# Norms of q and k taken in two steps and spread over reordered projection groups, in a transformer block on one core

## The chip, the core and the metric

The kernel runs on one core of one Trainium2 chip. The core has a matrix engine (TensorE, PE in the profile; its weight loads are PEld), a vector engine (VectorE, DVE), a scalar engine for activation functions (ScalarE, ACT), a general engine (GpSimd, POOL) and a queue that issues transfers (SyncE, SP). Each engine works through its own list of instructions in order and waits on semaphores. The metric is the device time of one execution in microseconds, the median of several runs.

## What is computed

One block with 256 tokens of width 2048, a context of 256 tokens, everything in float32:

```python
h  = modulate(rms_norm(x, norm1_w), sh1, sc1)          # hc the same from ctx
q, k, v, ft, pool, sv, sb, sc = split(h @ w_in)        # 5632 columns: 3 x 1024, then 5 x 512
kc, vc = split(hc @ w_in[:, 1024:3072])
q, k, kc = (rms_norm(per head of 128, weight) for each)
branches = (neighbourhood_attention(q, k, v, kc, vc, rpb), fourier_mix(ft),
            pool_mix(pool), short_conv_mix(sv, sb, sc))
x = x + g1 * (sum_i sigmoid(h @ w_gate[i]) * (branches[i] @ w_branch[i])) @ w_o
x = x + g2 * swiglu(modulate(rms_norm(x, norm2_w), sh2, sc2))
```

There are eight attention heads of width 128. The six modulation vectors come from `silu(c) @ w_mod + b_mod`.

## The kernel before

Every large product is made of three matmuls: weights and activations are split into a high and a low half (`split`), the high half cast by ScalarE (L90), the low half subtracted by VectorE (L91), and `mm3` adds high x high, high x low and low x high (L95 to L97). A weight tile of 128 x 1024 float32 (512 KB) holds two rows of 128 weights for 512 columns, or other shapes of this size. There are five buffers for raw weights and three each for the high and the low halves.

The input projection `h @ w_in` runs over the 16 blocks of 128 input rows in chunks of 1, 1, 2, 4, 4 and 4. In each chunk `in_groups` goes over the columns and adds its part into the tiles `xin[0..10]` (512 columns each: 0 and 1 are q, 2 and 3 are k, 4 and 5 are v, 6 Fourier, 7 pooling, 8 to 10 convolution) and, for columns 2 to 5 alone, into `cin[2..5]` for the context. In the last chunk `last(g)` finishes one group of 512 columns: two weight tiles (in the profile in_0 and in_2, their halves in_0h, in_0l, in_2h, in_2l), 24 matmuls for x (in_psx) and, for groups 2 to 5, 24 more for the context (in_psc). A finished product is added into its tile by VectorE (L301). `last` also calls `pump` twice, which issues one job of the queue `jobs` for every second call: a load of a modulation weight tile and, three jobs later, its sum on VectorE (`mod_sum`, L386).

`qk_norm` normalizes one tile of 4 heads: a square on ScalarE (L447), a sum per head on VectorE (L450), a small scale and offset on VectorE and the power -1/2 on GpSimd (`rstd_of`, L243 and L244), and the scaling of the whole tile on VectorE (L452). It is called for q0, k0 and ck0 (heads 0 to 3) after the groups 0, 2 and 4, and for q1, k1 and ck1 (heads 4 to 7) after group 10.

`bias_pair` fills the position bias of two heads by eight small transfers that GpSimd issues, and adds a mask on GpSimd (L470). `head(h, bias)` is one attention head: transposes of q, k and ck, scores, softmax, transposes of the weights, and the product with v. Heads 0 to 3 are called among the groups, heads 4 to 7 among the gates that follow. `fourier` (L537 to L545) comes after the groups, then `gate(0, 1, ...)`, whose weights are the tiles gt.

All tiles of 128 x 1024 that live longer (inputs, scratch for squares, the heads' tiles, biases) share 34 buffers, `U`. The order of each engine's list isn't the order of the program: a planner goes through the program with its own costs of each instruction, prefers what stands earlier in the program among the instructions that it takes to be ready, and hands out buffers as they come free. `tc.issue_after(ins)` adds an order without a wait: what is issued in the block comes behind `ins` on its engine. `state["low"]` is the last subtraction of `split` (L91) that the program has written so far.

Of the kernel before, what the change touches and what calls it, by code (L numbers as in the profile page):

```python
# [8 lines left out]
F32 = mybir.dt.float32  # L9
F32R = mybir.dt.float32r  # L10
AF = mybir.ActivationFunctionType
ALU = mybir.AluOpType
# [3 lines left out]
P = 128  # L16
# [26 lines left out]
def block_kernel(ctx: ExitStack, tc: tile.TileContext, t_in, out):  # L43
    nc = tc.nc
# [6 lines left out]
    sm = ctx.enter_context(tc.tile_pool(name="sm", bufs=1))  # L51
# [3 lines left out]
    def U(name, dtype=F32):  # L55
        return up.tile([P, 1024], dtype, tag="u", name=name, bufs=NU)
# [7 lines left out]
    def tr_ps(name):  # L64
        return pst.tile([P, 512], F32, tag="tr", name=name)
# [61 lines left out]
    def tsplit(hi, lo, src):  # L127
        nc.scalar.copy(hi, src)
        nc.vector.tensor_tensor(lo, src, hi.bitcast(F32), ALU.subtract)
# [3 lines left out]
    state = {"tick": 0, "every": 2, "hold": False, "low": None}  # L133

    def pump():
        state["tick"] += 1
        if state["tick"] % state["every"] == 0 and jobs and not state["hold"]:
            jobs.pop(0)()
# [102 lines left out]
    def rstd_of(ss, out_, n, scale):  # L241

        nc.vector.tensor_scalar(ss, ss, scale, EPS, ALU.mult, ALU.add)  # L243
        nc.gpsimd.tensor_tensor(out_, ss, mhalf.to_broadcast([P, n]), ALU.pow)  # L244
# [46 lines left out]
    xin = [None] * 11  # L291
    cin = [None] * 6
# [10 lines left out]
    def in_groups(kt0, nk, c0, cw):  # L303

        first = kt0 == 0

        kn, cn = min(nk, 2), 1024 // min(nk, 2)
        done = {}
        for c in range(c0, c0 + cw, cn):
            pw = min(cn, c0 + cw - c)  # L310
            for ka in range(0, nk, kn):
                raw = raw_tile(f"in_w{kt0}_{c}_{ka}")
                rv = raw[:, :kn * pw].rearrange("p (k f) -> p k f", k=kn)
                r = (kt0 + ka) * P
                nc.sync.dma_start(
                    rv, w_in[r:r + kn * P, c:c + pw].rearrange("(k p) f -> p k f", p=P))
                wh, wl = split(rv, f"in{kt0}_{c}_{ka}", (kn, pw))
                for gc in range(0, pw, 512):
                    done.setdefault(c + gc, []).append(
                        (ka, ka + kn, wh[:, :, gc:gc + 512], wl[:, :, gc:gc + 512]))  # L320
        for gc, parts in done.items():
            g = gc // 512
            for which in ("x", "c") if 2 <= g < 6 else ("x",):
                store = xin if which == "x" else cin
                if first:
                    store[g] = U(f"in_{which}{g}").rearrange("p (t f) -> p t f", t=NT)
                for t in range(NT):
                    ps = acc_ps(f"in_ps{which}{kt0}_{g}_{t}")
                    sl = slice(t * P, (t + 1) * P)
                    for ka, kb, wh, wl in parts:  # L330
                        for kk in range(ka, kb):
                            hi, lo = hx(kt0 + kk) if which == "x" else hc[kt0 + kk]
                            mm3(ps, hi[:, sl], lo[:, sl], wh[:, kk - ka, :], wl[:, kk - ka, :],
                                kk == 0, kk == nk - 1)
                    evict(ps, store[g][:, t, :], first, (g + t) % 2)
# [105 lines left out]

    def qk_norm(buf, name):
        v3 = buf.rearrange("p t (h d) -> p (t h) d", d=P)
        scr = U(f"sq_{name}")
        nc.scalar.activation(scr, buf.rearrange("p t f -> p (t f)"), AF.Square)  # L447
        ss = sm.tile([P, 8], F32, tag="ssh", name=f"ssh_{name}", bufs=2)
        rs = sm.tile([P, 8], F32, tag="rsh", name=f"rsh_{name}", bufs=2)
        nc.vector.tensor_reduce(ss, scr.rearrange("p (h d) -> p h d", d=P), AX.X, ALU.add)  # L450
        rstd_of(ss, rs, 8, 1.0 / P)
        nc.vector.tensor_tensor(v3, v3, rs.unsqueeze(2).to_broadcast([P, 8, P]), ALU.mult)  # L452

    rpb = t_in["rpb"]
    wmask = const.tile([P, GRID_W], F32, name="wmask")
# [2 lines left out]
    def bias_pair(h0):  # L458


        b = U(f"bias{h0}").rearrange("p (h t f) -> p h t f", h=2, t=NT)
        for i in range(2):
            for r in range(ROWS):
                src = bass.AP(rpb.tensor, rpb.offset + (h0 + i) * 15 * 31 + (7 - r) * 31 - 48,
                              [[1, GRID_W], [31, ROWS], [1, GRID_W]])
                p0 = (r % 2) * GRID_W
                nc.gpsimd.dma_start(
                    b[p0:p0 + GRID_W, i, r // 2, :].rearrange("p (a c) -> p a c", a=ROWS), src)
        bv = b.rearrange("p h t (a c) -> p (h t a) c", a=ROWS)
        nc.gpsimd.tensor_tensor(  # L470
            bv, bv, wmask.unsqueeze(1).to_broadcast([P, 2 * NT * ROWS, GRID_W]), ALU.add)
        return b

    def reverse(v):

        return v.rearrange("p (r c) -> p r c", c=GRID_W)[:, :, ::-1]

    def head(h, bias):
        g, o_ = h // 4, (h % 4) * P

        qf = U(f"qf{h}")
        pa, pb = tr_ps(f"qk_ps{h}"), tr_ps(f"ck_ps{h}")
        for t in range(NT):
            nc.tensor.transpose(pa[:, t * P:(t + 1) * P], xin[g][:, t, o_:o_ + P], ident)
            nc.tensor.transpose(pa[:, S + t * P:S + (t + 1) * P], xin[2 + g][:, t, o_:o_ + P], ident)
            nc.tensor.transpose(pb[:, t * P:(t + 1) * P], cin[2 + g][:, t, o_:o_ + P], ident)

        nc.scalar.mul(qf[:, 0:S].rearrange("p (r c) -> p r c", c=GRID_W), reverse(pa[:, 0:S]), qks[:, 0:1])
        nc.vector.tensor_scalar(qf[:, S:2 * S], pa[:, S:2 * S], qks[:, 1:2], None, ALU.mult)
        nc.scalar.mul(qf[:, 2 * S:3 * S], pb[:, :S], qks[:, 1:2])  # L490
        p_ = U(f"p{h}").rearrange("p (t f) -> p t f", t=NT)
        pT = U(f"pT{h}").rearrange("p (j q) -> p j q", j=4)
        for t in range(NT):
            sl = slice(t * P, (t + 1) * P)
            s_ps = tr_ps(f"s_ps{h}{t}")
            nc.tensor.matmul(s_ps, lhsT=qf[:, sl], rhs=qf[:, S:3 * S], start=True, stop=True)
            nc.vector.tensor_tensor(s_ps[:, :S], s_ps[:, :S], bias[:, t, :], ALU.add)
            nmx = sm.tile([P, 1], F32, tag="nmx", name=f"nmx{h}{t}", bufs=2)
            nc.vector.tensor_reduce(nmx, s_ps, AX.X, ALU.max, negate=True)
            sm_ = sm.tile([P, 1], F32, tag="sum", name=f"sum{h}{t}", bufs=2)  # L500
            nc.scalar.activation(p_[:, t, :], s_ps, AF.Exp, bias=nmx, scale=1.0, accum_out=sm_)
            rc = sm.tile([P, 1], F32, tag="rc", name=f"rc{h}{t}", bufs=2)
            nc.vector.reciprocal(rc, sm_)
            nc.vector.tensor_scalar(p_[:, t, :], p_[:, t, :], rc, None, ALU.mult)
            p_ps = tr_ps(f"p_ps{h}{t}")
            for j in range(4):
                nc.tensor.transpose(p_ps[:, j * P:(j + 1) * P], p_[:, t, j * P:(j + 1) * P], ident)
            nc.scalar.copy(pT[:, :, sl], p_ps.rearrange("p (j q) -> p j q", j=4))
        o_ps = tr_ps(f"o_ps{h}")
        for j in range(4):  # L510
            v_ = xin[4 + g] if j < 2 else cin[4 + g]
            nc.tensor.matmul(o_ps[:, :S], lhsT=v_[:, j % 2, o_:o_ + P], rhs=pT[:, j, :],
                             start=j == 0, stop=j == 3)
        hi, lo = bT[0][h // 4]
        tsplit(hi[:, h % 4, :].rearrange("p (r c) -> p r c", c=GRID_W),
               lo[:, h % 4, :].rearrange("p (r c) -> p r c", c=GRID_W), reverse(o_ps[:, :S]))
# [146 lines left out]
    def last(g):  # L663
        in_groups(starts[-1], CHUNKS[-1], g * 512, 512)
        for _ in range(2):
            pump()

    bt_tiles(0, 2)
    for g in (0, 2, 4):
        last(g)  # L670
    qk_norm(xin[0], "q0")
    qk_norm(xin[2], "k0")
    qk_norm(cin[2], "ck0")
    bias = bias_pair(0)
    head(0, bias[:, 0])
    last(1)
    head(1, bias[:, 1])
    last(3)
    bias = bias_pair(2)
    head(2, bias[:, 0])  # L680
    last(5)
    head(3, bias[:, 1])
    for g in (6, 7, 8, 9, 10):
        last(g)
        if g == LOAD_AT:
            load_tables()
    qk_norm(xin[1], "q1")
    qk_norm(xin[3], "k1")
    qk_norm(cin[3], "ck1")
    bias = bias_pair(4)  # L690
    fourier()
    load_pool()
# [192 lines left out]
```

## Time and profile before

| | us |
|---|---|
| median of 3 runs (lowest, highest) | 1789.87 (1789.64, 1791.45) |
| the profiled execution | 1791.95 |
| its span, from the first instruction to the last | 1790.2 |
| TensorE busy in the span | 1746.6 (98%) |
| VectorE busy | 1139.6 (64%) |
| ScalarE busy | 741.5 (41%) |
| GpSimd busy | 63.5 (4%) |

The mean clock that was granted to TensorE is 0.996 of full speed. In the rows of a timeline the first number is the start, the second the duration, both in us; then engine, line, operation, the tile written and the tiles read, and in brackets how long the engine had been idle before and what ended that. Durations of neighbouring instructions overlap by about 0.1 us on VectorE and by more on TensorE, where matmuls are pipelined: there the distance of the starts (0.23 us for a matmul of 512 columns) is what one costs. The last chunk's groups lie between 325.9 and 435.2 us.

### The profile page before, as it was taken

How to read it: one execution, taken by the hardware profiler on the slowest of the kernel's cores; microseconds unless marked ns; L12 is line 12 of the kernel's file. 1: busy time of each engine (PE TensorE's matmuls, PEld its weight loads, DVE VectorE, ACT ScalarE, POOL GpSimd, SP SyncE). 2: the span in 40 equal slices, each digit the busy share in tenths (PEclk: the TensorE clock that was granted, in tenths of full speed). 3: DMA queues.
4: the chain of work that ended last, by engine and by line, in shares of the span. 5: the costliest groups of instructions: out<-in, count | busy, mean ns of one | idle time of the engine just before them, and what ended most of it. 6: DMA issues, size and time to landing. Idle time of an engine off the chain costs nothing.

```text
span 1790.2 us, 20871 instructions
## 1 busy us (share of the span) xinstructions
PE 1746.6 (98%) x7874; PEld 1397.0 (78%) x7874; DVE 1139.6 (64%) x1310; ACT 741.5 (41%) x870; POOL 63.5 (4%) x78
## 2 busy tenths in 40 slices
PE   5999999998999999999999999999999999999998
PEld 3676877776777888888888778888888888888887
DVE  5875656677778677777777567776544444454544
ACT  5322322334455444444444454444444444433342
POOL 0000000223010000000000000000000000000000
PEclk9999999999999999999999999999999999999999
DMA  9786675667776788888998548887556666565663
GB/s 315 251 283 224 194 252 178 138 131 185 235 188 226 259 275 290 286 288 262 308 319 286 185 153 281 283 283 227 182 188 188 189 190 189 190 201 197 208 203 116
DMA packets 212872, 404.06 MB, mean 226 GB/s; under 512 B 14178, under 2 KB 53012, under 8 KB 212772
## 3 DMA queue, kind: packets, MB, share of 16 engines
q1 hardware_dynamic: 209732, 396.37, 68.1%
q0 software_dynamic: 1888, 4.26, 2.4%
q10 hardware_dynamic: 1152, 2.10, 0.3%
q8 instruction: 62, 1.02, 0.2%
q14 instruction: 38, 0.31, 0.0%
HBM read 400.58 MB, written 2.10 MB: 225 GB/s over the span
## 4 chain that ended last, share of the span: by engine, by line
PE 72%; issue 2%; DVE 1%; DMA 0%; ACT 0%; POOL 0%; POOLq 0%; DVEq 0%; ACTq 0%
PE gt_ps L96 6%; PE gt_ps L97 6%; PE gt_ps L95 6%; PE fu_ps L97 4%; PE fu_ps L95 4%; PE fu_ps L96 4%; PE dn_ps L97 4%; PE dn_ps L95 4%; PE dn_ps L96 4%; PE fg_ps L95 4%; PE fg_ps L97 4%; PE fg_ps L96 4%; PE br_ps L95 2%; PE br_ps L96 2%; PE br_ps L97 2%
## 5 line engine op out<-in xcount | busy, mean ns | idle before, releaser
L386 DVE SCALAR_TENSOR_TENSOR macc<-mod,cs,macc 128x1024 f32<-128x1024 f32 x128 | 163.8, 1280 | 0.0
L301 DVE TENSOR_TENSOR in_x<-in_x,in_psx 128x512 f32<-128x512 f32 x110 | 74.2, 684 | 40.3 <-PE in_psx L97 39.9
L90 ACT CAST in_2h<-in_w 128x1024 fp32r<-128x1024 f32 x33 | 34.7, 1052 | 148.5 <-PE in_psc L97 94.6
L95 PE MATMUL in_psx<-in_0h,hxh 128*128 128x512 f32 x220 | 89.1, 412 | 1.3 <-ACT hxh L281 1.0
L90 ACT CAST in_0h<-in_w 128x1024 fp32r<-128x1024 f32 (+1 forms) x56 | 57.8, 1035 | 77.3 <-PE in_psc L97 36.9
L96 PE MATMUL in_psx<-in_0l,hxh 128*128 128x512 f32 x220 | 87.1, 399 | 0.0
L97 PE MATMUL in_psx<-in_0h,hxl 128*128 128x512 f32 x220 | 86.6, 396 | 0.0
L91 DVE TENSOR_TENSOR in_0l<-in_w,in_0h 128x1024 fp32r<-128x1024 f32 (+1 forms) x56 | 69.5, 1241 | 3.4 <-ACT in_0h L90 3.3
L91 DVE TENSOR_TENSOR in_2l<-in_w,in_2h 128x1024 fp32r<-128x1024 f32 x33 | 40.4, 1224 | 34.3 <-ACT in_2h L90 32.5
L95 PEld LDWEIGHTS in_psx<-in_0h,hxh 128*128 128x128 f32 x220 | 41.5, 191 | 24.9 <-issue 6.7
L96 PE MATMUL in_psx<-in_2l,hxh 128*128 128x512 f32 x132 | 53.4, 405 | 3.7 <-DVE in_2l L91 3.7
L95 PE MATMUL in_psx<-in_2h,hxh 128*128 128x512 f32 x132 | 53.4, 404 | 0.0
L97 PE MATMUL in_psx<-in_2h,hxl 128*128 128x512 f32 x132 | 51.9, 393 | 0.0
L96 PEld LDWEIGHTS in_psx<-in_0l,hxh 128*128 128x128 f32 x220 | 42.1, 191 | 10.7 <-issue 1.7
L97 PEld LDWEIGHTS in_psx<-in_0h,hxl 128*128 128x128 f32 x220 | 42.2, 192 | 9.1
L209 PE MATMUL mod_ps<-mod_w,cst 128*32 128x512 f32 (+1 forms) x288 | 40.9, 580 | 4.6 <-DMA mod_w<-in_w_mod 4.6
L301 DVE TENSOR_TENSOR in_c<-in_c,in_psc 128x512 f32<-128x512 f32 x40 | 27.2, 686 | 22.7 <-PE in_psc L97 22.6
L91 DVE TENSOR_TENSOR gt_0l<-gt_w,gt_0h 128x1024 fp32r<-128x1024 f32 x16 | 19.6, 1224 | 25.9 <-ACT gt_0h L90 25.9
L96 PEld LDWEIGHTS in_psx<-in_2l,hxh 128*128 128x128 f32 x132 | 24.9, 189 | 11.7 <-DVE in_2l L91 4.5
L91 DVE TENSOR_TENSOR br_0l<-br_w,br_0h 128x1024 fp32r<-128x1024 f32 x16 | 19.6, 1225 | 22.3 <-ACT br_0h L90 22.3
L91 DVE TENSOR_TENSOR gt_12l<-gt_w,gt_12h 128x1024 fp32r<-128x1024 f32 x16 | 19.6, 1225 | 20.3 <-ACT gt_12h L90 20.3
L96 PE MATMUL in_psc<-in_0l,hch 128*128 128x512 f32 x80 | 31.2, 390 | 0.0
(657 smaller groups left out, 5171.4 us busy)
## 6 DMA issues: line engine op xcount, KB each, us to landing
mod<-in_w_mod SPq DMA_DIRECT2D x128, 512.0 KB, 5.5
gt_w<-in_w_gate SPq DMA_DIRECT2D x128, 512.0 KB, 5.5
fg_w<-in_w_ffn_gate SPq DMA_DIRECT2D x88, 512.0 KB, 4.2
fu_w<-in_w_ffn_up SPq DMA_DIRECT2D x88, 512.0 KB, 3.5
dn_w<-in_w_ffn_down SPq DMA_DIRECT2D x88, 512.0 KB, 4.7
in_w<-in_w_in SPq DMA_DIRECT2D x87, 512.0 KB, 5.1
mod_w<-in_w_mod SPq DMA_DIRECT2D x128, 256.0 KB, 5.2
wo_w<-in_w_o SPq DMA_DIRECT2D x32, 512.0 KB, 5.3
```

The costliest lines, as they stand in the source:

```text
L90: nc.scalar.copy(hv, src)
L91: state["low"] = nc.vector.tensor_tensor(lv, src, hv.bitcast(F32), ALU.subtract)
L95: nc.tensor.matmul(ps, lhsT=xh, rhs=wh, start=first, stop=False)
L96: nc.tensor.matmul(ps, lhsT=xh, rhs=wl, start=False, stop=False)
L97: nc.tensor.matmul(ps, lhsT=xl, rhs=wh, start=False, stop=last)
L209: nc.tensor.matmul(ps[32 * j:32 * j + 32, :2 * nf], lhsT=cst[:, kk, :], rhs=rvs[j // kn][:, j % kn, :, :].rearrange("p s f -> p (s f)"), s ...
L301: nc.vector.tensor_tensor(dst, dst, ps, ALU.add)
L386: nc.vector.scalar_tensor_tensor(macc[m][h_], mod_raw.pop((m, kk, h_)), cs[:, 0, kk:kk + 1], macc[m][h_], ALU.mult, ALU.add)
```

## The change

`qk_norm` becomes two functions. `qk_rstd` does the square, the sums and the power; `qk_scale` scales the tile, ordered behind the last low-half subtraction written so far. The small tiles get three buffers in place of two. The groups come in the order 2, 0, 4, 3, 1, 5, 6 to 10 in place of 0, 2, 4, 1, 3, 5, 6 to 10. The norms of both sets are spread over the groups, the first bias pair is asked for earlier, and the heads 0 to 3 come one group later in the program.

```diff
-    def qk_norm(buf, name):
-        v3 = buf.rearrange("p t (h d) -> p (t h) d", d=P)
+    def qk_rstd(buf, name):
         scr = U(f"sq_{name}")
         nc.scalar.activation(scr, buf.rearrange("p t f -> p (t f)"), AF.Square)
-        ss = sm.tile([P, 8], F32, tag="ssh", name=f"ssh_{name}", bufs=2)
-        rs = sm.tile([P, 8], F32, tag="rsh", name=f"rsh_{name}", bufs=2)
+        ss = sm.tile([P, 8], F32, tag="ssh", name=f"ssh_{name}", bufs=3)
+        rs = sm.tile([P, 8], F32, tag="rsh", name=f"rsh_{name}", bufs=3)
         nc.vector.tensor_reduce(ss, scr.rearrange("p (h d) -> p h d", d=P), AX.X, ALU.add)
         rstd_of(ss, rs, 8, 1.0 / P)
-        nc.vector.tensor_tensor(v3, v3, rs.unsqueeze(2).to_broadcast([P, 8, P]), ALU.mult)
+        return buf, rs
+
+    def qk_scale(buf, rs):
+        v3 = buf.rearrange("p t (h d) -> p (t h) d", d=P)
+        with tc.issue_after(state["low"].ins):
+            nc.vector.tensor_tensor(v3, v3, rs.unsqueeze(2).to_broadcast([P, 8, P]), ALU.mult)
...
     bt_tiles(0, 2)
-    for g in (0, 2, 4):
-        last(g)
-    qk_norm(xin[0], "q0")
-    qk_norm(xin[2], "k0")
-    qk_norm(cin[2], "ck0")
+    last(2)
+    k0, ck0 = qk_rstd(xin[2], "k0"), qk_rstd(cin[2], "ck0")
     bias = bias_pair(0)
+    last(0)
+    qk_scale(*k0)
+    q0 = qk_rstd(xin[0], "q0")
+    qk_scale(*ck0)
+    last(4)
+    qk_scale(*q0)
+    last(3)
     head(0, bias[:, 0])
+    k1, ck1 = qk_rstd(xin[3], "k1"), qk_rstd(cin[3], "ck1")
     last(1)
+    qk_scale(*k1)
     head(1, bias[:, 1])
-    last(3)
+    q1 = qk_rstd(xin[1], "q1")
     bias = bias_pair(2)
+    last(5)
+    qk_scale(*ck1)
     head(2, bias[:, 0])
-    last(5)
+    last(6)
+    qk_scale(*q1)
     head(3, bias[:, 1])
-    for g in (6, 7, 8, 9, 10):
+    for g in (7, 8, 9, 10):
         last(g)
         if g == LOAD_AT:
             load_tables()
-    qk_norm(xin[1], "q1")
-    qk_norm(xin[3], "k1")
-    qk_norm(cin[3], "ck1")
     bias = bias_pair(4)
     fourier()
```

## The prediction

> **What bounds the kernel now.** I read the page first (engines' shares), then who waited for whom on TensorE (PE) around the norms, then the clock by stretches, then the timelines of VectorE (DVE), GpSimd (POOL) and ScalarE (ACT) in the two places that stood out.
>
> ```profile
> span 1790.2 us, 20871 instructions
> ...
> PE 1746.6 (98%) x7874; PEld 1397.0 (78%) x7874; DVE 1139.6 (64%) x1310; ACT 741.5 (41%) x870; POOL 63.5 (4%) x78
> ```
>
> PE is busy for 98% of the span, so a change that removes no matmul can only win time in which PE stands idle or runs at a lower clock. Between 325 and 460 us, where both sets of norms lie, PE waited so:
>
> ```profile
> PE in_psx L96 <- DVE in_2l L91: 3.7, 2, 3.1
> PE ft_o L543 <- ACT ft_a L540: 2.7, 1, 2.7
> PE gt_ps L96 <- DVE gt_0l L91: 2.6, 1, 2.6
> ```
>
> Columns: total us, number of waits, longest. So there are four waits: 3.1 us (3.11 in the timeline), 0.56, 2.73 and 2.60. The clock behind them, by stretches (length, busy us of PE, PEld, DVE, ACT, POOL, granted clock, DMA share, GB/s):
>
> ```profile
> 325.92:331.36 5.44, 5.44 (x26) 4.50 (x25) 3.65 (x5) 2.11 (x2) 0.00 (x0) 1.00 0.65 200
> 348.50:352.00 3.50, 3.50 (x11) 2.67 (x10) 1.93 (x4) 0.00 (x0) 1.42 (x1) 0.51 1.21 37
> 435.20:441.70 6.50, 3.77 (x11) 2.14 (x10) 1.22 (x2) 1.53 (x2) 2.90 (x2) 0.92 0.59 211
> 441.70:452.20 10.50, 7.90 (x16) 4.35 (x15) 7.88 (x7) 1.33 (x3) 5.84 (x3) 0.72 0.16 53
> 1041.30:1043.00 1.70, 1.70 (x8) 1.52 (x9) 0.51 (x2) 0.76 (x2) 0.00 (x0) 0.54 0.73 242
> 1043.00:1046.00 3.00, 3.00 (x16) 2.82 (x15) 2.23 (x7) 2.12 (x6) 0.00 (x0) 0.69 0.30 114
> ```
>
> The first row is one projection group on x (5.44 us); a group on x and context takes two such passes. The second row lies just behind the 3.11 us wait: clock 0.51 for 3.50 us, which loses 3.50 x 0.49 = 1.7 us more. The third and fourth lose 6.50 x 0.08 + 10.50 x 0.28 = 3.5 us. The last two are far away, behind this wait:
>
> ```profile
> 1041.29 1.02 PE L766 MATMUL h_tp<-ident,xn 128*128 128x128 f32 x4 [2.08 <-ACT xn L759]
> ```
>
> They lose 1.70 x 0.46 + 3.00 x 0.31 = 1.7 us. So a single wait of 2.08 us already brings the slow clock, and a wait costs its length and about 1.7 us.
>
> **First place.** DVE's timeline, from the scaling of q on:
>
> ```profile
> 337.92 1.23 DVE L452 TENSOR_TENSOR in_x<-in_x,rsh_q 128x1024 f32<-128x1024 f32 x1 [1.79 <-POOL rsh_q L244]
> 339.06 0.68 DVE L301 TENSOR_TENSOR in_x<-in_x,in_psx 128x512 f32<-128x512 f32 x1
> 340.88 1.22 DVE L450 TENSOR_REDUCE ssh_k<-sq_k 128x8 f32<-128x1024 f32 x1 [1.13 <-ACT sq_k L447]
> 342.01 0.68 DVE L301 TENSOR_TENSOR in_c<-in_c,in_psc 128x512 f32<-128x512 f32 x1
> 342.61 0.17 DVE L243 TENSOR_SCALAR ssh_k<-ssh_k 128x8 f32<-128x8 f32 x1
> 344.53 1.22 DVE L452 TENSOR_TENSOR in_x<-in_x,rsh_k 128x1024 f32<-128x1024 f32 x1 [1.76 <-POOL rsh_k L244]
> 345.67 0.68 DVE L301 TENSOR_TENSOR in_c<-in_c,in_psc 128x512 f32<-128x512 f32 x1
> 346.27 1.22 DVE L91 TENSOR_TENSOR in_2l<-in_w,in_2h 128x1024 fp32r<-128x1024 f32 x1
> ```
>
> DVE works in order. The scaling (L452) stands idle 1.76 us for POOL's power, and behind it stands in_2l, the low half of the second weight pair of the group that PE is in. An undisturbed in_2l has this margin (DVE's row, then PE's use of it):
>
> ```profile
> 331.28 1.23 DVE L91 TENSOR_TENSOR in_2l<-in_w,in_2h 128x1024 fp32r<-128x1024 f32 x1 [1.76 <-ACT in_2h L90]
> ```
> ```profile
> 332.94 0.39 PE L96 MATMUL in_psx<-in_2l,hxh 128*128 128x512 f32 x1
> ```
>
> It ends at 331.28 + 1.23 = 332.51, PE wants it at 332.94: 0.43 us to spare. Anything longer ahead of it is an idle PE.
>
> **Second place.** POOL, DVE and ACT at the end of the projections:
>
> ```profile
> 438.80 2.34 POOL L470 TENSOR_TENSOR bias<-bias,wmask 128x1024 f32<-128x1024 f32 x1 [5.41 <-issue]
> 441.10 1.66 POOL L244 TENSOR_TENSOR rsh_k<-ssh_k,mhalf 128x8 f32<-128x8 f32 x1
> 442.74 2.33 POOL L575 TENSOR_TENSOR in_x<-in_x,in_x 128x1024 f32<-128x1024 f32 x1
> ```
> ```profile
> 442.79 3.36 DVE L452 TENSOR_TENSOR in_x<-in_x,rsh_k 128x1024 f32<-128x1024 f32 x1 [6.37 <-POOL rsh_k L244]
> 446.08 0.16 DVE L243 TENSOR_SCALAR ssh_ck<-ssh_ck 128x8 f32<-128x8 f32 x1
> 446.15 1.21 DVE L91 TENSOR_TENSOR gt_0l<-gt_w,gt_0h 128x1024 fp32r<-128x1024 f32 x1
> ```
> ```profile
> 438.69 1.04 ACT L90 CAST gt_4h<-gt_w 128x1024 fp32r<-128x1024 f32 x1 [3.59 <-DMA gt_w<-in_w_gate]
> 439.64 0.58 ACT L540 COPY ft_a<-ft_ps 128x512 f32<-128x512 f32 x1
> ```
>
> k1's power stands in POOL's queue behind the masking of a bias pair, which started only after 5.41 us of idling ("issue": no releaser is seen; I read it as the pair's transfers); DVE's scaling waits 6.37 us for it, and gt_0l, which PE needs, stands behind the scaling. That is PE's 2.60. The 2.73 is another matter: ft_a's copy stands on ACT behind a cast whose weights had not landed.
>
> **The change, part by part.** *Counts.* The six norms keep all their instructions: six squares, reductions (1.22, row of 340.88), small scalings (0.17), powers (1.66, row of 441.10) and scalings (1.23). A square is
>
> ```profile
> L447 ACT ACTIVATE sq_q<-in_x x2: 1053/1058/1063, 333.1 to 423.3; 128x1024 f32<-128x1024 f32 x2
> ```
>
> Nothing is added or removed, so 0 us by count; one more buffer for the two small tiles costs no time, bounded by one power's wait (1.76) either way.
>
> *First set split.* k0 now takes q0's old place in time: its x pass ends first, its power is ready near 337.9 as q0's was. Its scaling must come behind in_2l of group 0, due at about 336.7 (0.08 before group 0 starts at 336.80) and done at 337.9. So DVE finds the power there: no wait. ck0 and q0 follow a group later. I count the first place as removed: -3.11 - 1.7 = -4.81. Bounds: 0 (it returns, first rival) and -4.81.
>
> *Second set moved.* k1, q1 and ck1 are reduced and scaled among groups 1, 5 and 6. Their three powers leave the queue ahead of bias pair 4's masking, and gt_0l no longer stands behind a scaling. Of the second place, 2.73 + 2.60 + 3.5 = 8.8 us in all, I leave the ft_a wait and its slow clock (2.73 + 1.7 = 4.4): the gain is -4.4. Bounds: 0 and -8.8.
>
> By the Trainium skill, "TensorE: Matmul & The Clock Gate", section "What's actually happening", PE falls to half clock after at least one idle window of about 3.4 us. By that rule the 2.73 left alone would bring no slow clock, the gain here would be 8.8 - 2.73 = 6.1 and the time 1.7 us lower. The trace differs, 2.08 us of idling having sufficed at 1041.29, so I stay with 4.4.
>
> *Heads later.* Head 0 starts behind group 3 in place of group 4, so one 10.9 us group later. The four heads are a chain that took from
>
> ```profile
> 358.14 0.27 PE L484 MATMUL qk_ps<-ident,in_x 128*128 128x128 f32 x1
> ```
> ```profile
> 430.47 1.03 PE L512 MATMUL o_ps<-pT,in_c 128*128 128x256 f32 x4
> ```
>
> that is 73.3 us. Starting at 364.0 (325.92 + 7 x 5.44) it ends near 437, while the projections, 4.8 + 0.6 us shorter, would end near 430 where they ended at 435.2 (the start of the third stretch above, with the Fourier step). The 7 us of overhang lie beside the first gate's matmuls, which need no head: 16 weight rows x 2 token halves x 3 = 96, four passes of 24, so 4 x 5.44 = 22 us. I take 0; without that cover it is +7.
>
> *bias_pair(0).* Its eight transfers and the mask are issued five passes (27 us) before head 0 instead of directly before. Before, mask and split met:
>
> ```profile
> 360.48 3.30 POOL L470 TENSOR_TENSOR bias<-bias,wmask 128x1024 f32<-128x1024 f32 x1 [6.39 <-DMA bias<-in_rpb]
> ```
> ```profile
> 361.43 3.43 DVE L91 TENSOR_TENSOR in_0l<-in_w,in_0h 128x1024 fp32r<-128x1024 f32 x1
> ```
>
> A subtraction of 1.22 took 3.43, and the 0.56 us wait came of it. The mask will meet some other DVE instruction, so I take 0, between -0.56 and 2.2 - 0.43 = +1.8 (if it is an in_2l). The Trainium skill, "Advanced Engine Details and Errata", section "Mode Summary", has GpSimd and VectorE blocking each other on a shared second port. The trace agrees (3.43 and 3.36 against 1.22); by that rule the +1.8 is the likelier end wherever mask and in_2l coincide.
>
> *DVE more crowded.* 3 x (1.22 + 0.17 + 1.23) = 7.9 us of norm work move from the end into groups 1 to 6. DVE was busy 3.65 of 5.44 us in a bare group, so 1.8 are free in each, before any head's work. Some in_2l will come late as the 0.56 did; I take two: +1.1. Bounds: 0, and +8.1 for three cases of 2.7 (1.0 of wait and 1.7 of slow clock).
>
> *SP's queue.* The order of w_in's columns changes, not their number. In the last groups
>
> ```profile
> 423.57 7.84 SPq L109 DMA_DIRECT2D gt_w<-in_w_gate  x3
> ```
>
> the gate's loads go out as raw buffers come free, paced by the splits, so they move with PE: 0; if they do not, the second rival below.
>
> Sum: -4.8 - 4.4 + 0 + 0 + 1.1 = -8.1 us. The profiled execution took 1791.95 us, so 1783.9 against itself; it lies 2.1 above the median of the runs, 1789.87, which gives 1781.8.
>
> **Rivals.** *The first place returns at ck0.* ck0's scaling is held only behind in_2l of group 0; q0's squares are written before it, but group 4 is not. ck0's x-context pass ends at 336.8, exactly when k0's did before, so its power is ready near 344, and in_2l of group 4 is due at 342.2. If DVE's queue has the scaling first, 344.53's row happens again: 4.8 comes back, 1786.6. For it: the very same timing; against: the scheduler must again think the power ready earlier than the cast.
>
> *The last wait moves.* PE comes to the Fourier step 4.8 us earlier while the weights of gt_4h land when they did (438.69's row): ft_a's wait grows by what the first place gave, 1786.6 too, up to 1789.9 if gt_0l's place is taken over. Against: the loads are paced by PE.
>
> *All goes.* With DVE free of norms at the end, gate and Fourier work order themselves so that ft_a's wait goes too: -8.1 - 4.4, 1777.4.
>
> *Slower: the mask ahead of a power, among the groups.* In POOL's queue bias pair 0's mask may stand ahead of q0's power, and pair 2's ahead of k1's or q1's, as pair 4's did of k1's. Each costs DVE 6.37 of idling and 3.36 - 1.23 of holding = 8.5, and now an in_2l stands behind, not one gate weight: less DVE's 1.76 us of slack and the 0.43, 6.3 us of PE and 1.7 of slow clock, 8.0. One such place gives 1789.8, two 1797.8; it decides from 5.9 us each on. Against: in the first set before, the powers stood ahead of the mask.
>
> **How the numbers follow.** Forecast 0.42; ck0's return 0.18; the moved wait 0.12; all goes 0.15; mask ahead of power 0.13. Faster by over 0.2% (3.6 us, about what a measurement here can tell from no change): the forecast, all goes, and somewhat under half of the two cases at 1786.6, 0.64. Within: the rest of those and the single mask, 0.20. Slower: two masks, or crowding at its upper bound over a partial gain, 0.16. The likeliest's own range is 1779 to 1785; for eight in ten, 1776 to 1793.
>
> **What would show it.** Right: no L452 row with a POOL wait and an in_2l behind; PE's list for the stage without the 3.1 and the gt_0l wait; one ft_a wait of 2 to 3 us with a clock near 0.5 behind it; DVE's squares, reductions and scalings of k1, q1, ck1 between groups 1 and 7. Wrong: a power behind L470 on POOL with a scaling waiting for it; the in_psx L96 group over 3.7 us in all; ft_a's wait over 5 us; or a difference outside 325 to 460 us, where I expect none.

## The result, and the profile after

The changed kernel is slower: 1806.7 us (median; lowest 1805.75, highest 1809.22) against 1790.12, a ratio of 1.0096 [1.0084, 1.0107], so 16.6 us more. Its profiled execution took 1805.75 us with a span of 1804.0 and a mean clock of 0.994 (before: 1791.95, 1790.2, 0.996).

What PE waited for between 320 and 480 us in the kernel after (total us, number of waits, longest):

```profile
PE in_psx L96 <- DVE in_2l L91: 12.0, 3, 8.9
PE ft_ps L542 <- DMA dft_l<-in_dft_l: 8.6, 1, 8.6
PE in_psx L96 <- DVE in_0l L91: 2.9, 2, 2.1
PE p_ps L512 <- DVE p L509: 1.5, 1, 1.5
PE s_ps L501 <- DVE qf L494: 0.3, 1, 0.3
```

The four waits of before (3.11, 0.56, 2.73 and 2.60 us, 9.0 together) are gone, and eight others of 25.4 us stand in their place: 8.86, 8.58, and six small ones of 7.91 together. (in_psx, in_0l and in_2l belong to the input projection, ft_ps and dft_l to the Fourier step and its table, s_ps, qf, p_ps and p to the attention heads.) Lines have moved by five: scaling is L457, bias transfers L472, the mask L475.

**The 8.86 us wait.** GpSimd, VectorE and TensorE in the kernel after, then the clock behind the wait (a row by stretch, with columns as in the prediction):

```profile
343.78 1.28 POOL L472 DMA_DIRECT2D bias<-in_rpb  x2
356.18 2.33 POOL L475 TENSOR_TENSOR bias<-bias,wmask 128x1024 f32<-128x1024 f32 x1 [11.12 <-DMA bias<-in_rpb]
358.48 1.66 POOL L244 TENSOR_TENSOR rsh_q<-ssh_q,mhalf 128x8 f32<-128x8 f32 x1
...
346.72 0.17 DVE L243 TENSOR_SCALAR ssh_q<-ssh_q 128x8 f32<-128x8 f32 x1
...
360.18 1.23 DVE L457 TENSOR_TENSOR in_x<-in_x,rsh_q 128x1024 f32<-128x1024 f32 x1 [11.57 <-POOL rsh_q L244]
...
361.92 1.22 DVE L91 TENSOR_TENSOR in_2l<-in_w,in_2h 128x1024 fp32r<-128x1024 f32 x1
...
363.19 0.79 PE L96 MATMUL in_psx<-in_2l,hxh 128*128 128x512 f32 x1 [8.86 <-DVE in_2l L91]
```
```profile
363.20:367.00 3.80, 3.80 (x10) 3.03 (x11) 3.47 (x4) 0.00 (x0) 0.00 (x0) 0.60 0.63 170
```

The sums for q0's power are ready at 346.72 + 0.17 = 346.89. GpSimd's next instruction is the mask of bias pair 0, which waits 11.12 us for the pair's transfers; the power follows at 358.48, 11.6 us late. On VectorE the scaling of q0 waits for it, in_2l stands behind the scaling, and TensorE waits for in_2l. The slow clock costs some 1.6 us more.

**The 8.58 us wait.** SP's list in the kernel after, TensorE's row, and the place that the same transfer had before:

```profile
444.46 4.86 SPq L109 DMA_DIRECT2D gt_w<-in_w_gate  x2
...
450.64 1.83 SPq L528 DMA_DIRECT2D dft_l<-in_dft_l  x1
...
468.92 3.53 PE L542 MATMUL ft_ps<-dft_l,in_x 128*128 128x512 f32 x4 [8.58 <-DMA dft_l<-in_dft_l]
```
```profile
415.95 0.42 SPq L523 DMA_DIRECT2D dft_l<-in_dft_l  x1
```

The Fourier table's load, issued at 415.95 before and long there when it was needed, now stands behind the eighth gate weight at 450.64 and lands 18 us later. The list of waits of SP names what held its issue, which I read as a buffer that head 3's scores give back:

```profile
SPq L528 <- PE s_ps L501: 1.6, 1, 1.6
```

Most of the later issue is the place in the list; 1.6 us is only the wait there. But the place alone would not have made TensorE wait: it asks for the table at 460.34 (468.92 - 8.58), and in a run below (e3), where the same load goes out at 419.75, it lands within 4.2 us. Here GpSimd issues the eight transfers of bias pair 4 between 447.78 and 452.67, and the load takes 18.1 us. From issue to landing, the kernel after and then e3:

```profile
DMA to landing us min/median/max: 18.1/18.1/18.1
```
```profile
DMA to landing us min/median/max: 4.2/4.2/4.2
```

From 448 to 452 and from 452 to 456 us the DMA engines are busy for 0.81 and 0.98 of the time and move 33 and 159 GB/s. No run separates the late place from this company.

**Six small waits around the heads 0 to 3.** The largest two, 2.70 and 2.14 us, with what stands ahead of them:

```profile
398.74 1.23 DVE L457 TENSOR_TENSOR in_x<-in_x,rsh_k 128x1024 f32<-128x1024 f32 x1 [1.36 <-POOL rsh_k L244]
...
400.82 1.22 DVE L457 TENSOR_TENSOR in_c<-in_c,rsh_ck 128x1024 f32<-128x1024 f32 x1
...
402.55 1.22 DVE L91 TENSOR_TENSOR in_2l<-in_w,in_2h 128x1024 fp32r<-128x1024 f32 x1
...
424.20 0.43 DVE L502 TENSOR_TENSOR s_ps<-s_ps,bias 128x256 f32<-128x256 f32 x1 [2.67 <-POOL bias L475]
```
```profile
413.52 2.56 POOL L244 TENSOR_TENSOR rsh_q<-ssh_q,mhalf 128x8 f32<-128x8 f32 x1 [8.97 <-DVE ssh_q L243]
416.04 0.65 POOL L472 DMA_DIRECT2D bias<-in_rpb  x1
421.77 2.40 POOL L475 TENSOR_TENSOR bias<-bias,wmask 128x1024 f32<-128x1024 f32 x1 [5.08 <-issue]
```

Two scalings of the second set stand ahead of in_2l (2.70, with the clock at 0.59 between 403.80 and 408.00). And q1's power, for which GpSimd idles 8.97 us, holds back the eighth transfer of bias pair 2 until 416.04, so that the mask comes late, head 2's bias addition waits 2.67 us for it, and an in_0l behind that is 2.14 late.

Account: + 8.86 + 1.6 (clock) + 8.58 + 1.6 + 7.91 + 1.7 = 30.2; gone are 9.0 of waits and the slow clock behind three of them, 1.7 + 3.5 = 5.2. That makes 16.0 in this stretch. The medians differ by 16.6, but the two profiled executions, from which these rows are, by 13.8: outside the stretch the kernel before lost more, 1.4 us in a wait at its start (8.1 against 6.7) and some 2.1 around 1041 us, where its wait of 2.08 brought the slow clock and the kernel after's of 1.69 did not. About 1 us stays open.

### The profile page after: what moved, and what is told of

It reads as the page before. It is cut to its first block, busy times and chain, and to the rows that moved or that the text cites. A ratio compares the mean times of both kernels' runs of the same rounds, so it can differ in the third digit from the quotient of the medians.

```text
span 1804.0 us, 20877 instructions
## 1 busy us (share of the span) xinstructions
PE 1745.6 (97%) x7874; PEld 1395.3 (77%) x7874; DVE 1135.9 (63%) x1310; ACT 740.2 (41%) x870; POOL 62.6 (3%) x78
## 4 chain that ended last, share of the span: by engine, by line
PE 71%; issue 2%; DMA 1%; DVE 1%; ACT 0%; POOL 0%; POOLq 0%; DVEq 0%; ACTq 0%
PE gt_ps L96 6%; PE gt_ps L97 6%; PE gt_ps L95 6%; PE fu_ps L97 4%; PE fu_ps L95 4%; PE fu_ps L96 4%; PE dn_ps L95 4%; PE dn_ps L97 4%; PE dn_ps L96 4%; PE fg_ps L95 4%; PE fg_ps L97 4%; PE fg_ps L96 4%; PE br_ps L95 2%; PE br_ps L96 2%; PE br_ps L97 2%
## 5 line engine op out<-in xcount | busy, mean ns | idle before, releaser
L95 PEld LDWEIGHTS in_psx<-in_0h,hxh 128*128 128x128 f32 x220 | 41.7, 192 | 25.4 <-issue 6.9
L96 PEld LDWEIGHTS in_psx<-in_2l,hxh 128*128 128x128 f32 x132 | 25.4, 193 | 20.4 <-DVE in_2l L91 13.4
```

What stands on the lines that cost most here:

```text
L95: nc.tensor.matmul(ps, lhsT=xh, rhs=wh, start=first, stop=False)
L96: nc.tensor.matmul(ps, lhsT=xh, rhs=wl, start=False, stop=False)
```

## The experiments

My theory: two thirds of the new loss come from two orders in queues, the mask ahead of q0's power (10.5 us with the clock) and the table's load behind the gate's (10.2); the two steps of the norms themselves do what the prediction said. Rivals: that the regrouping and the later heads cost the time, whatever the queues hold (then undoing the two orders would move the waits and not the time); and that the split alone, in the old order, is what wins or loses.

**e1: the first bias pair asked for later** (in the kernel after)

```diff
     k0, ck0 = qk_rstd(xin[2], "k0"), qk_rstd(cin[2], "ck0")
-    bias = bias_pair(0)
     last(0)
...
     qk_scale(*q0)
+    bias = bias_pair(0)
     last(3)
```

> The changed kernel with one edit: bias_pair(0) is asked for after q0's power instead of before it, so that in GpSimd's list q0's power stands ahead of the pair's last two transfers and its mask. Theory (two separate losses: a power behind a mask on GpSimd, tables late in SyncE's list): the 8.86 us wait of TensorE and its 1.6 us of slow clock go, about 10.5 us, 1806.7 to about 1796; the 8.6 us wait for the DFT tables stays. Rival 1 (VectorE is overcrowded in groups 0 to 4 whatever GpSimd does): an in_2l or in_0l wait of 3 us or more stays in 340 to 370 us and the gain is under 5 us. Rival 2 (the projections merely end earlier, and the tables' wait grows by as much): the table wait grows from 8.6 to about 17 us and the time stays at 1804 to 1807.

Measured: 1798.81 us, 1.0046 [1.003, 1.0061], 7.9 less than the kernel after. GpSimd now has the power first:

```profile
349.19 1.66 POOL L244 TENSOR_TENSOR rsh_q<-ssh_q,mhalf 128x8 f32<-128x8 f32 x1 [1.13 <-DVE ssh_q L243]
...
363.53 2.40 POOL L475 TENSOR_TENSOR bias<-bias,wmask 128x1024 f32<-128x1024 f32 x1 [11.44 <-DMA bias<-in_rpb]
```

and the 8.86 is gone; the table's wait stays (8.41). Some of the 10.5 comes back. The wait for in_0l near head 2, 2.15 us (2.14 in the kernel after, with no slow clock behind it), now brings the slow clock, 1.7. And in_2l, at 345.55 behind ck0's scaling, is late by 1.04, without a slow clock; 10.5 - 1.7 - 1.0 = 7.8:

```profile
344.40 1.23 DVE L457 TENSOR_TENSOR in_c<-in_c,rsh_ck 128x1024 f32<-128x1024 f32 x1 [1.17 <-POOL rsh_ck L244]
...
346.82 0.50 PE L96 MATMUL in_psx<-in_2l,hxh 128*128 128x512 f32 x1 [1.04 <-DVE in_2l L91]
```

**e2: the tables loaded ahead of head 3** (in the kernel after)

```diff
+    load_tables()
     head(3, bias[:, 1])
     for g in (7, 8, 9, 10):
         last(g)
-        if g == LOAD_AT:
-            load_tables()
```

> The changed kernel with one edit: load_tables is called ahead of head 3 in place of behind group 8, so the DFT tables get their two long-lived buffers before head 3's tiles do and stand in SyncE's list where they stood before the change (behind the second gate weight). Theory (two separate losses): the 8.6 us wait of the Fourier matmul for the tables goes, and its slow clock of some 2 us, 1806.7 to about 1796; q0's wait (8.86) stays. Rival (the tables' wait is only where TensorE would have waited anyway, for head 3, which is late): another wait of 5 us or more stands between 440 and 475 us, and the time stays above 1802.

Measured: 1796.6 us, 1.0036 [1.0023, 1.005], 10.1 less than the kernel after. No wait for dft_l is left; in_2l's 9.0 stays. What made the load late is its place behind head 3 and two groups in the program; the edit takes it away from bias pair 4's transfers as well.

**e3: both edits together**

> The edits of the two other kernels together (bias_pair(0) after q0's power; tables ahead of head 3). Theory: the two losses add, about 21 us in all, 1806.7 to about 1786, a few us below the kernel before (1790.1), because its two stalls are gone as predicted and the crowding of VectorE around heads 1 and 2 (waits of 2.7 and 2.1 us) is left. Rival (moving the norms among the heads costs what it saves): what remains is at or above 1790.

Measured: 1788.08 us, 0.9987 [0.9977, 0.9996]: 18.6 less than the kernel after, where 7.9 + 10.1 make 18.0. The two losses add up, and undoing them takes back more than the whole difference, so the rival that blames the regrouping for it is out. TensorE's waits in the same stretch:

```profile
PE in_psx L96 <- DVE in_2l L91: 4.2, 3, 2.7
PE in_psx L96 <- DVE in_0l L91: 2.8, 2, 2.1
PE p_ps L512 <- DVE p L509: 1.5, 1, 1.5
PE s_ps L501 <- DVE qf L494: 1.0, 2, 0.7
```

Neither gt_0l nor ft_a is among them: the second place of the prediction is gone altogether. What is left, 9.5 us, are the small waits around the heads and the 1.04 of e1.

**e6 and e12: the second set's steps behind the heads** (the same kernel in both; the profile shown is that of e12)

```diff
 # e3, and from the groups 3, 1, 5 and 6 the six calls for k1, ck1, q1 go to:
+    last(7)
+    k1 = qk_rstd(xin[3], "k1")
+    last(8)
+    qk_scale(*k1)
+    ck1 = qk_rstd(cin[3], "ck1")
+    last(9)
+    qk_scale(*ck1)
+    q1 = qk_rstd(xin[1], "q1")
+    last(10)
+    qk_scale(*q1)
```

> The kernel with both mendings (bias_pair(0) after q0's power; tables ahead of head 3), and the second set of norms moved out of the heads' stretch: k1 reduced behind group 7, ck1 behind 8, q1 behind 9, each scaled a group later in the program. Theory (the waits of 2.7, 0.75, 0.5 and 2.1 us around heads 1 and 2 come of the second set among the heads: two scalings ahead of an in_2l, and bias pair 2's last transfer behind q1's power, which makes its mask and head 2 late): they go, with 1.7 us of slow clock, and 1788.1 becomes about 1781. Rival (VectorE is crowded there by the heads themselves, which now meet groups of one pass): waits of 4 us or more in all stay between 390 and 430 us, and the time stays above 1785.

> The kernel with both mendings and the second set late once more, for its profile. Theory: 1783.5 within 1 us; the waits of 2.7, 0.75, 0.5 and 2.1 us around heads 1 and 2 are gone, and what is left between 320 and 470 us sums to under 4 us. Rival (they moved and are paid elsewhere): waits of 5 us or more remain in that stretch.

Measured: 1783.52 us, 0.9963 [0.9949, 0.9977], and 1783.14, 0.9965 [0.9953, 0.9978]. This version beats both kernels, by about 7 and 23.5 us; 1781 was expected. The waits of e12:

```profile
PE s_ps L501 <- DVE qf L494: 3.1, 2, 2.1
PE gt_ps L96 <- DVE gt_4l L91: 2.2, 1, 2.2
PE in_psx L96 <- DVE in_2l L91: 1.0, 1, 1.0
```

6.3 us in place of 9.5, where under 4 was expected. The 2.70 and the 2.14 are gone; a smaller gt_4l behind the scalings and a qf behind a slowed sum came. That sum is the modulation's, and it runs while the mask does:

```profile
402.48 3.48 DVE L386 SCALAR_TENSOR_TENSOR macc<-mod,cs,macc 128x1024 f32<-128x1024 f32 x1
```
```profile
402.48 2.39 POOL L475 TENSOR_TENSOR bias<-bias,wmask 128x1024 f32<-128x1024 f32 x1 [13.11 <-DMA bias<-in_rpb]
```

(1.28 us elsewhere). The medians lie 4.6 to 4.9 apart; these two profiles account for 3.2 of idling, less the slow clock (some 1.7 us) behind one more wait, and e12's profiled execution (1787.21) lies above its own median, e3's (1786.11) below. That the later place is better is measured; the remainder of its gain isn't traced.

**e4: the kernel before, with bias pair 4 asked for behind the Fourier step**

```diff
-    bias = bias_pair(4)
     fourier()
     load_pool()
+    bias = bias_pair(4)
```

> The kernel before with one edit: bias_pair(4) is asked for after the Fourier step instead of ahead of it, so the powers of q1 and k1 stand ahead of any of its transfers and its mask in GpSimd's list. The prediction's term for the second place says that gt_0l's wait (2.60 us) and half of the slow clock there came of the mask ahead of k1's power: 1790.1 to about 1786, with ft_a's wait of 2.7 us left. Rival (the wait was the gate weight's own lateness): gt_0l's wait stays within 0.5 us of 2.6, time unchanged. A later bias pair could also make head 4 wait for its bias, which would give some of it back; that would show as DVE waiting for L470 at head 4.

Measured: 1793.71 us, 1.0016 [1.0006, 1.0026], where 1786 was expected. The mask that stood ahead of k1's power is out of the way, and gt_0l's wait falls from 2.60 to 0.57. ft_a's falls too, from 2.73 to 0.2, which was not expected, and the mask does not explain it (see e7). ft_a's copy stood behind the cast of gt_4h, whose weight was late (438.69 in the prediction's row). In the kernel before seven of pair 4's transfers are issued from 415.12 on, beside the gate's loads; in e4 they are not. The third gate weight, that of gt_4h, goes out at 423.57 before and at 424.02 in e4. From there to its landing, before and then e4, with e4's cast:

```profile
DMA to landing us min/median/max: 15.0/15.0/15.0
```
```profile
DMA to landing us min/median/max: 4.4/4.4/4.4
...
435.88 1.04 ACT L90 CAST gt_4h<-gt_w 128x1024 fp32r<-128x1024 f32 x1 [0.30 <-PE in_psx L97]
```

From 424 to 428 us the DMA engines moved 188 GB/s before and 279 in e4. So the two waits of the second place hang on the same bias pair in two ways: one on its mask in GpSimd's list, the other on its transfers. But now the pair is late for head 4:

```profile
461.94 2.33 POOL L470 TENSOR_TENSOR bias<-bias,wmask 128x1024 f32<-128x1024 f32 x1 [13.92 <-DMA bias<-in_rpb]
```
```profile
468.31 1.11 PE L507 MATMUL p_ps<-ident,p 128*128 128x128 f32 x4 [9.54 <-DVE p L504]
```

**e5: the first set alone in two steps, groups in the old order** (in the kernel before)

```diff
-    for g in (0, 2, 4):
-        last(g)
-    qk_norm(xin[0], "q0")
-    qk_norm(xin[2], "k0")
-    qk_norm(cin[2], "ck0")
+    last(0)
+    q0 = qk_rstd(xin[0], "q0")
+    last(2)
+    qk_scale(*q0)
+    k0, ck0 = qk_rstd(xin[2], "k0"), qk_rstd(cin[2], "ck0")
+    last(4)
+    qk_scale(*k0)
+    qk_scale(*ck0)
     bias = bias_pair(0)
```

> The kernel before, its groups and heads in their old order, with only the first set of norms in two steps: q0 reduced behind group 0 and scaled behind group 2's low halves, k0 and ck0 reduced behind group 2 and scaled behind group 4's low halves; bias_pair(0) after all powers; the second set as before. Theory (the prediction's first term is right by itself, and what spoiled it were the mask ahead of q0's power and the later heads and tables): the 3.1 us wait for in_2l and its 1.7 us of slow clock go, the second place stays: 1790.1 to about 1785.3. Rival (two steps put the load on VectorE elsewhere): new in_2l or in_0l waits of 2 us or more between 336 and 365 us, time within 2 us of 1790.

Measured: 1793.6 us, 1.0024 [1.0014, 1.0034], where 1785.3 was expected. The split does its work: in_2l goes at 342.70, ahead of k0's scaling at 345.46. The 3.1 is gone, and 7.65 has come further on. The pair's last transfers went out behind ck0's power, as before and 1.5 us earlier, yet the mask ran at 364.80 in place of 360.48, after 12.19 us of idling in place of 6.39 (why the transfers took longer was not tried); head 0's bias addition waited for it, with an in_2l behind:

```profile
364.80 2.33 POOL L480 TENSOR_TENSOR bias<-bias,wmask 128x1024 f32<-128x1024 f32 x1 [12.19 <-DMA bias<-in_rpb]
...
367.17 0.43 DVE L507 TENSOR_TENSOR s_ps<-s_ps,bias 128x256 f32<-128x256 f32 x1 [9.23 <-POOL bias L480]
...
369.97 0.79 PE L96 MATMUL in_psx<-in_2l,hxh 128*128 128x512 f32 x1 [7.65 <-DVE in_2l L91]
```

So in the old order the split alone isn't a gain either: the bias is what comes late next.

**e7: e5, and the second set's three powers ahead of its three scalings**

```diff
-    qk_norm(xin[1], "q1")
-    qk_norm(xin[3], "k1")
-    qk_norm(cin[3], "ck1")
+    k1, ck1, q1 = qk_rstd(xin[3], "k1"), qk_rstd(cin[3], "ck1"), qk_rstd(xin[1], "q1")
+    qk_scale(*k1)
+    qk_scale(*ck1)
+    qk_scale(*q1)
     bias = bias_pair(4)
```

> The kernel before with the first set in two steps as in the kernel that does this alone, and the second set still at the end, but all three powers (k1, ck1, q1) issued first and the three scalings held behind the last low halves; group and head order as before. In GpSimd's list k1's and ck1's powers now stand ahead of bias pair 4's mask, q1's behind it. Theory: the first place goes (4.8 us) and gt_0l's wait goes or shrinks (2.6 us and its half of the slow clock, 1.7), ft_a's stays: 1790.1 to about 1781. Rival (q1's power behind the mask holds VectorE just as k1's did): gt_0l's wait is 2 us or more, time about 1785.

Measured: 1793.57 us, 1.0017 [1.0008, 1.0026], the same as e5, where 1781 was expected. in_2l's wait is 8.19, ft_a's 3.58, gt_0l's 2.26: at the end q1's power fell behind the mask in k1's place. Which norm stands behind the mask changes, the wait for gt_0l hardly does, as the rival said. ft_a's stays although two of the three powers are ahead of the mask: pair 4's transfers are still issued beside the gate's loads (from 417.90 on), and gt_4h's weight takes 15.9 us to land.

**e8, e9, e10, e11: the first bias pair asked for far earlier.** In e8 (the kernel before) `bias_pair(0)` is written ahead of the first three norms; in e9 (e5), e10 (the kernel after) and e11 (e6) it is written ahead of the whole last chunk:

```diff
     bt_tiles(0, 2)
+    bias = bias_pair(0)
...
-    bias = bias_pair(0)
```

> The kernel before with one edit that adds the suspected cost: bias_pair(0) is asked for ahead of the norms of the first set, so its eight transfers and its mask stand ahead of all three powers in GpSimd's list, as the mask stood ahead of q0's power in the changed kernel. Theory (a mask that waits for its transfers ahead of a power stops VectorE): the scaling of q0 waits for GpSimd until the transfers have landed; if they are issued when q0's scaling falls due, near 336 us, and land 12 us later as in the changed kernel, the wait for in_2l grows from 3.1 to about 10 us and the time from 1790 to about 1797. If instead the transfers are issued as soon as the buffer is free, several us before 330, the mask is over before the power is due and nothing changes; then the time stays within 2 us of 1790, and what decides is when the transfers start, not the order alone.

> The kernel before, groups and heads in their old order, with the first set of norms in two steps (as in the kernel that does this alone) and bias_pair(0) asked for ahead of the whole last chunk. In the kernel that does the first set alone the wait moved to head 0, whose bias mask came 12 us after the pair's last transfer, itself behind ck0's power. Theory: with the pair out of the way nothing is left to wait for, so the prediction's first term shows by itself: the waits of 3.1 and 0.56 us for in_2l go with 1.7 us of slow clock, and the time is about 1785 (1790.2 less 5.4). Rival (two steps load VectorE elsewhere whatever GpSimd does): in_2l or in_0l waits of 2 us or more in 336 to 375 us, time above 1788.

> The changed kernel with bias_pair(0) asked for ahead of the whole last chunk, and nothing else. Theory (what stopped VectorE was the mask's wait of some 12 us for its transfers, in front of q0's power): all of q0's wait goes, more cleanly than when the pair was only moved behind q0's power, which left a 1.04 us wait: 1806.7 to about 1795.5; the tables' wait (8.4 to 8.6) stays. Rival (the order of power and mask alone matters, and any place behind the power would do as well): the same time as there, 1798.8, within 1 us.

> Both mendings, the second set of norms behind the heads, and bias_pair(0) ahead of the whole last chunk. Theory: the kernel with the second set late took 1783.5; the wait of about 1 us for in_2l in group 4 that the pair's place behind q0's power left goes too: about 1782.5, with no wait of TensorE over 2 us between 320 and 470 us. Rival (the last waits are the heads' own): no change within 0.7 us.

Measured: e8 1790.66 us, 1.0003 [0.9994, 1.0012]; e9 1793.16, 1.0018 [1.0008, 1.0027]; e10 1809.05, 1.0111 [1.0097, 1.0126]; e11 1790.54, 1.0006 [0.9998, 1.0015]. Expected were 1785, 1795.5 and 1782.5 for e9, e10 and e11. In the stage of the norms the long waits go, though e10 and e11 keep the 1.04 us wait for in_2l that they were meant to remove. e9's whole list between 320 and 480 us is

```profile
PE ft_o L553 <- ACT ft_a L550: 2.7, 1, 2.7
PE gt_ps L96 <- DVE gt_0l L91: 2.4, 1, 2.4
PE p_ps L517 <- DVE p L514: 0.3, 1, 0.3
```

so the first place and its follower are both gone, and in e10 the 8.86 is. But the planner issued the eight transfers at once, at 137 us in e9, into a stretch where the DMA engines were busy all the time already. Before and e9, the same 5 us (clock, DMA share and GB/s are the last three columns), and TensorE's rows behind it:

```profile
145.00:150.00 5.00, 5.00 (x24) 3.43 (x23) 2.59 (x3) 1.04 (x1) 0.00 (x0) 1.00 1.01 334
```
```profile
145.00:150.00 5.00, 5.00 (x26) 3.77 (x21) 2.15 (x3) 0.71 (x2) 0.00 (x0) 1.00 1.05 136
155.00:160.00 5.00, 3.41 (x8) 0.43 (x8) 0.28 (x1) 1.04 (x1) 0.00 (x0) 0.50 1.04 356
...
155.82 3.41 PE L209 MATMUL mod_ps<-mod_w,cst 128*32 128x512 f32 x8 [3.64 <-DMA mod_w<-in_w_mod]
```

The DMA engines are as busy and move 136 GB/s in place of 334; a modulation weight is 3.64 us late, another 0.93, and with the clock at 0.50 for 8.25 busy us (3.41 of them here, 4.84 in the next 5 us) about 8.7 us are lost. Against 5.3 saved among the norms (waits of 5.4 in place of 9.0, and 1.7 of clock) that makes +3.4; measured is +2.9. The other three pay in the same way. The first power of the last chunk comes 9.5 us later in e9 than in the kernel before (345.71 and 336.22), 8.0 later in e10 than in the kernel after, 13.6 in e11 than in e12 (e11's profiled execution was the longest of its twelve) and 3.4 in e8 than before. In e8 the transfers went out at 204 us and the mask was over long before the first power, so that neither the case that the edit was meant to make (a mask ahead of a power) nor a gain came of it: in_2l's 3.1 is still there.

## Why the prediction was wrong

*First place, −4.8: right.* The wait of 3.11 is gone in the kernel after, in e5 and in e9. In the kernel after in_2l goes first, and the scaling of k0 finds its power there, with no wait:

```profile
336.17 1.23 DVE L91 TENSOR_TENSOR in_2l<-in_w,in_2h 128x1024 fp32r<-128x1024 f32 x1 [1.50 <-ACT in_2h L90]
...
337.91 1.22 DVE L457 TENSOR_TENSOR in_x<-in_x,rsh_k 128x1024 f32<-128x1024 f32 x1
```

*Second place, −4.4 of 8.8: too small.* With the powers out of the mask's way gt_0l's wait went, as counted. I left ft_a's 2.73 as "another matter", and that was the error: it came of bias pair 4's transfers beside the gate's loads, and went where the pair moved (e4, and e3, where the pair goes out at 438.88 and gt_4h is cast at 435.58). "All goes" had the effect, but for a reason that e4 shows not to be needed.

*bias_pair(0), 0 between −0.56 and +1.8: the first step that failed.* I looked at what the mask would collide with on VectorE and not at what stands behind it on GpSimd. It is the slower rival in one place, pair 0's mask ahead of q0's power, with 8.86 + 1.6 where I had priced 6.3 + 1.7; e1 takes back 7.9. I gave it 0.13 because "in the first set before, the powers stood ahead of the mask". But there the pair was written behind all three norms, and here it is written ahead of q0's. The order of the program, which the planner prefers where it takes both to be ready, had changed just there.

*SP's queue, 0, and Heads later, 0: the second step that failed.* I took only the w_in and gate loads and let them move with TensorE. The tables' loads take long-lived buffers from `U`, which the heads hold; with the heads a group later, their place in SP's list went behind eight gate loads and into the company of bias pair 4's transfers, 8.58 + 1.6 us. e2 takes back 10.1. The overhang of the heads showed no cost of its own: what it cost was the loads ordered behind it.

*DVE more crowded, +1.1: the term that was mis-sized.* Six waits of 7.91 and 1.7 of clock, 9.6, above my upper bound of 8.1. I had let the free 1.8 us in each bare group stand for the groups in which a head runs too. Part of it is no crowding: the 2.14 came of bias pair 2's last transfer behind q1's power, the reverse of the order that my slower rival had. With the same count of instructions e12 has waits of 6.3 where e3 has 9.5, so the place sets part of it.

*Rivals.* "The first place returns at ck0": not in the kernel after, where in_2l went ahead at 342.58; in e1, e3 and e10 to e12 it does, at 1.04 us with no slow clock, not at 4.8. "The last wait moves": no ft_a wait is left to grow. The working of the chances has two slips: with both gains lost and the crowding kept the time is 1791.0 and not 1789.9; and 0.42 + 0.15 and somewhat under half of 0.30 make about 0.70 and not 0.64. Neither would have put the forecast near 1806.7.

*Clock.* "A wait costs its length and about 1.7" is right for most waits from about 2.1 us on, though the price went from none to 3.0, and for none of the small ones (below).

## What to carry to other kernels

On an in-order engine a short, urgent instruction takes on the wait of whatever long one is written ahead of it: for every step that is moved, read down each engine's list, the two transfer queues included, and ask what now stands in front of what. A step that asks for transfers early must also be checked at the place where they go out, since small transfers can make the loads beside them late (e4, e9). Where an edit removes a wait and the time rises, look for the next late thing in the same queue: here undoing two orders (e3) and moving the second set behind the heads (e6) turned +16.6 us into −7.

## What the runs showed of the hardware

**No one length of wait decides the slow clock.** TensorE's rows of the kernel after, e5 and e12: the first two waits were followed by a granted clock of 1.00 for 4 us, the third, the shortest, by one of 0.50 between 1.5 and 4 us on.

```profile
428.20 0.50 PE L96 MATMUL in_psx<-in_0l,hxh 128*128 128x512 f32 x1 [2.14 <-DVE in_0l L91]
```
```profile
445.16 1.13 PE L553 MATMUL ft_o<-ft_a,dft_d 128*128 128x256 f32 x4 [3.35 <-ACT ft_a L550]
```
```profile
407.96 1.10 PE L501 MATMUL s_ps<-qf 128*128 128x512 f32 x2 [2.10 <-DVE qf L494]
```

In the profiles of before, after and every run but e6, between 320 and 480 us, waits of up to 1.52 us never brought it; of 35 waits from 2.08 us on, 32 did, and the others were these two and one of 2.08 in e3. Nor does the length of the wait set the price: behind 8.86 us it was 1.6 and behind 2.70 it was 1.7, but 2.5 behind 7.65 (e5), 2.7 behind 9.04 (e2) and 3.0 behind 2.98 (e8). The Trainium skill ("TensorE: Matmul & The Clock Gate", "What's actually happening") asks for an idle window of about 3.4 us. The trace differs: of the three rows here, all below that, the shortest brought the slow clock, and the shortest such wait among the 32 was 2.09 us (e10).

**A pair's eight transfers of 64 KB take the DMA engines at a low rate, and loads beside them land late.** In the rows shown here the mask starts 11 to 14 us after the last of them was issued (11.12, 11.44, 12.19, 13.11 and 13.92), in the kernel before 6.39 in the first pair; in e9 they cut what the engines moved to two fifths (136 GB/s of 334). Beside them a Fourier table took 18.1 us to land in the kernel after, and 4.2 in e3, where it was apart from them; a gate weight took 15.0 in the kernel before, and 4.4 in e4. Why they are slow was not tried.
